# A two-block transformer step on one core: the last feature pair in token halves, with the final norm on all partitions

## The chip, the cores and the metric

The kernel runs on one core of one Trainium2 chip. The metric is the device time of one execution, in microseconds (us). Three runs of the kernel before took 2533.3, 2534.14 and 2535.93 us; the median is 2534.14 us.

## What is computed

Two blocks on 256 tokens of 2048 features. The first mixes tokens by forgetting attention and by an mLSTM, the second by a spatial gating unit and a gated linear recurrence (RG-LRU). Each is followed by a feed-forward net with a three-tap causal convolution, and each part adds its result to the residual stream x. The change touches only what comes last: the down projection of the second feed-forward net, its residual sum, and the final RMS norm.

```
def _rmsnorm(x, g):
    xf = x.astype(jnp.float32)
    y = xf * lax.rsqrt(jnp.mean(xf * xf, axis=-1, keepdims=True) + RMS_EPS)
    return (y * g.astype(jnp.float32)).astype(x.dtype)
...
    x = x + jnp.einsum('bsf,fd->bsd', jax.nn.gelu(gate) * val, ffn_w_down[l])
return _rmsnorm(x, final_g)
```

## The kernel before

x lies transposed on chip: features on the 128 partitions, tokens along the row. It is held as 8 feature pairs of [128, 2, 256] (two times 128 features, 256 tokens). All weights stream from memory once, in float32. `halves` (L193) loads 1 MB at a time on SP's queue and splits it: `hi` is the weight rounded to float32r by ScalarE (L207), `lo` the remainder by VectorE (L208). Operands are split the same way: a `Pair` holds [hi 256 | lo 256] columns for two tiles of the contraction. A block is four such tiles of weights; six blocks of hi and six of lo fit on chip (pool `wc`).

`proj_b` (L228) computes one output pair: for each tile k and each f of the two sets of 128 features, L239 multiplies hi weights with all 512 operand columns and L240 adds lo weights times the 256 hi columns. The result stands in PSUM as two halves of 256 columns whose sum is the product. Between blocks `tick` (L148) emits one step of each job that follows an earlier product, so that other engines work beside PE. Within an engine, instructions run in the order in which they are emitted (weights are emitted ahead of it).

`residual` (L667) runs eight products, one per output pair, and starts an `add_pair` job (L691) after each. In the last call, at the end of the second feed-forward net, the contraction has 24 tiles. `add_pair` copies one half out of PSUM (L698), adds both to x (L699, L700), squares the new x (L303) and adds the squares to `acc` on GpSimd (L309); for the last pair it also folds acc's two halves to 256 columns (L305 to L307). Then x is multiplied by the final gain (L712). `Norm.steps` (L311) sums acc over the partitions with a matmul by a column of ones, in token halves (L315), adds epsilon (L318), raises to the power -0.5 on GpSimd (L320), spreads the result along a diagonal (L325) and multiplies by ones, which puts the norm of each token on every partition (L326, copied at L328). `final` (L931) multiplies the eight pairs by it, five on VectorE (L939) and three on GpSimd (L937), and stores each with one transfer of 256 KB (L940), alternating between the queues of ScalarE and SP.

Of the kernel before, what the change touches and what calls it, by code (L numbers as in the profile page):

```python
# [9 lines left out]
AF = mybir.ActivationFunctionType  # L10
# [50 lines left out]
class Job:  # L61
    """Work that follows a matrix product, emitted in steps between later products."""

# [10 lines left out]
class Pair:  # L74
    """Two K tiles of an operand: [128, 2, hi 256 | lo 256], written by a job."""

# [4 lines left out]
class Builder:  # L81
# [17 lines left out]

# [1 line left out]
    def _name(self, s):  # L101
# [26 lines left out]
    @staticmethod  # L128
    def half(quads, j):
        """Feature pair j of x: [128, 2, 256]."""  # L130
        return quads[j // 2][:, 2 * (j % 2):2 * (j % 2) + 2, :]
# [4 lines left out]

# [1 line left out]
    def soon(self, gen):  # L138
# [9 lines left out]
    def tick(self):  # L148
        """Between blocks of a product: every urgent job that is due takes a step, and one other."""
        for j in list(self.urgent):  # L150
            if j.wait <= 0:
                j.step()
            else:
                j.wait -= 1
        took = False
        for j in list(self.later):
            if j.wait <= 0 and not took:
                j.step()
                took = True
            else:  # L160
                j.wait -= 1
        self.urgent = [j for j in self.urgent if not j.done]
        self.later = [j for j in self.later if not j.done]
# [9 lines left out]

# [1 line left out]
    def constants(self):  # L175
# [15 lines left out]

# [1 line left out]
    def halves(self, src):  # L193
        """src: [128, k tiles, columns] in DRAM. Yields per block of k tiles its (hi, lo) parts,
        float32r tiles whose sum is the float32 weight."""
        nc = self.nc
        nk, ncol = src.shape[1], src.shape[2]
        with self.tc.high_priority(offset=self.ahead):
            raw = self.raw.tile([P, nk, ncol], F32, tag="raw", name=self._name("raw"))
            nc.sync.dma_start(out=raw, in_=src)  # L200
            step = 1024 // ncol
            out = []
            for k0 in range(0, nk, step):
                kn = min(step, nk - k0)
                hi = self.wc.tile([P, kn, ncol], F32R, tag="wh", name=self._name("wh"))
                lo = self.wc.tile([P, kn, ncol], F32R, tag="wl", name=self._name("wl"))
                nc.scalar.copy(hi, raw[:, k0:k0 + kn, :])  # L207
                nc.vector.tensor_sub(lo, raw[:, k0:k0 + kn, :], hi.bitcast(F32))  # L208
                out.append([(hi[:, k, :], lo[:, k, :]) for k in range(kn)])
        return out  # L210

    def blocks(self, w, nk, first, before=None):
        """Loads the k tiles of w [128, nk, columns] piece by piece; yields blocks of parts."""
        k = 0
        size = 2048 // w.shape[2]
        sizes = list(first)
        while k < nk:
            n = min(sizes.pop(0) if sizes else size, nk - k)
            if before is not None:
                before(k, n)  # L220
            yield from self.halves(w[:, k:k + n, :])
            k += n
# [5 lines left out]
    def proj_b(self, w, pairs, first=(), before=None):  # L228
        """Transposed product with 256 weight columns, w [128, k tiles, 256]. PSUM [128, 2, 512];
        the product is the sum of its two 256-column halves."""  # L230
        nc = self.nc
# [14 lines left out]
    def proj_a(self, w, pairs):  # L246
        """Product with 512 weight columns, w [128, k tiles, 512], in token rows:
        PSUM [128 tokens, 2 halves, 512]."""
        nc = self.nc
# [24 lines left out]
    def split(self, dst, src, gains=None):  # L274
        """dst [128, 2, 512] float32r <- hi and lo parts of src [128, 2, 256] (times gains)."""
        nc = self.nc
# [10 lines left out]

# [1 line left out]
    class Norm:  # L289
        """1/rms per token of features that come in pairs [128, 2, 256]: r [128, 2] by token,  # L290
        bc [128, 256] on every partition."""

# [40 lines left out]
    def log1p_exp_neg_abs(self, x, t, e, w2, eng):  # L333
        """t = log(1 + exp(-|x|)) = 2 atanh(e / (2 + e)), e = exp(-|x|)."""
        nc = self.nc
# [12 lines left out]

# [1 line left out]
    def gates(self, pairs, norm):  # L350
        """Gate pre-activations, one row per head: 0-3 mLSTM forget, 4-11 forgetting attention,
        32-35 mLSTM input. Leaves what both recurrences need by token and by row."""
        nc = self.nc
# [64 lines left out]
    def qk_rows(self, ps, t, norm, g):  # L418
        """RMS norm over each head of 512 columns in token rows, then transposed to t."""
        nc = self.nc  # L420
# [24 lines left out]
    def rows_out(self, ps, out, c, norm, func, after=None):  # L445
        """512 columns in token rows: func(r * z)."""
        self.finish(norm.job)
        for m in range(2):
            s = slice(c * 512, (c + 1) * 512)
            self.nc.scalar.activation(out[m][:, s], ps[:, m, :], func, scale=norm.r[:, m:m + 1])  # L450
            if after is not None:
                self.nc.gpsimd.tensor_mul(out[m][:, s], out[m][:, s], after[:, s])
        yield 0
# [42 lines left out]
    def mlstm_head(self, h, q, k, v, gs, d, deps):  # L496
        """h_t = sum_s (q_t k_s) e^(a_s - c_t) v_s / max(|den|, e^-m_t), a = i - F, c = max(0, cummax a)."""
        nc = self.nc
# [45 lines left out]
    def first_operand(self, j, xs):  # L544
        """Pair j of x * gain from DRAM."""
        x = self.wk_tile([P, 2, S])
# [118 lines left out]

# [1 line left out]
    def residual(self, quads, w, groups, norm=None, gname=None, scales=None):  # L667
        """x += sum of operands @ w over groups (first k tile, pairs); w [8, 128, k tiles, 256].
        With norm, the new x's squares go to it and the pairs x * gain come back."""
        out = []  # L670
# [20 lines left out]
    def add_pair(self, quads, j, pss, scales, norm, gname, p):  # L691
# [16 lines left out]
        if norm is not None:  # L708
            norm.add(x, last=last)
            if p is None:  # L710
# [3 lines left out]

# [1 line left out]
    def ffn(self, quads, hx, norm, w_up, cw, cb, w_down, func, next_gain):  # L716
        nt = w_up.shape[0]
        npair = nt // 2
        for half in range(2):
# [10 lines left out]
            if half == 0:  # L730
                self.residual(quads, w_down, [(0, prods)])
        n = self.Norm(self, D)
        return self.residual(quads, w_down, [(2 * j0, prods)], n, next_gain), n

    def conv_pair(self, ps, y, norm, cw, cb, f0, nf, func=None):
        """Three-tap causal convolution over the tokens of two feature tiles."""
        nc = self.nc
# [20 lines left out]

# [1 line left out]
    def lru_scales(self):  # L760
        """-+ LRU_C * softplus(-lam) per channel."""
        nc = self.nc
# [33 lines left out]
    def lru_scan(self, xr, ra, ii, th, deps):  # L796
        """1 - a^2 = tanh(-log a) (1 + a^2); the state replaces xr."""
        nc = self.nc
# [131 lines left out]

    def final(self, quads, norm):  # L931
        nc, a = self.nc, self.a
        self.finish(norm.job)
        for j in range(8):
            x = self.half(quads, j)
            if j in (2, 5, 7):
                nc.gpsimd.tensor_mul(x, x, self.bc2(norm.bc))  # L937
            else:
                nc.vector.tensor_mul(x, x, self.bc2(norm.pb))  # L939
            (nc.sync if j % 2 else nc.scalar).dma_start(out=a["out"][:, 2 * j:2 * j + 2, :], in_=x)  # L940

    def build(self):
# [4 lines left out]
        hx, norm = self.mix2(x, hx, norm)  # L947
        _, norm = self.ffn(x, hx, norm, a["ffn_w_up_2"], "ffn_conv_w_2", "ffn_conv_b_2", a["ffn_w_down_2"],
                           AF.Gelu_apprx_tanh, None)
        self.finish_all()  # L950
        self.final(x, norm)

# [7 lines left out]
def _layout(i):  # L960
# [11 lines left out]
    def tiles(w, n):  # L972
        """[K, F] -> [F / n, 128, K / 128, n]"""
        w = np.asarray(w)
# [51 lines left out]
```

## Time and profile before

| what | us |
|---|---|
| median of three runs | 2534.14 |
| span of the profiled execution (first to last instruction) | 2531.7 |
| PE busy (share of the span) | 2485.9 (98%) |
| last pair's product, start to last matmul | 2497.58 to 2514.11 |
| rest of the program after it, to the span's end | 17.4 |

The profiled execution is one of its own; the page gives its span, which is 2.4 us under the median of the runs. Times in rows count from the span's start. PE is the matmul engine and PEld its weight loads, DVE is VectorE, ACT ScalarE, POOL GpSimd, SP SyncE; a q behind a name is that engine's queue of instructions, which issues transfers. A busy time of PE overlaps with the next matmul's, so steps are read from start to start. A float32 matmul leaves two records, a float32r matmul one. Idle time in square brackets is that of the engine before the instruction, with what ended it. The granted clock is a share of 2.4 GHz.

### The profile page before, as it was taken

The numbers are of one execution on the slowest core, as the hardware profiler recorded it, in microseconds if no ns is written. First come the engines' busy times: TensorE is split into PE (matmuls) and PEld (weight loads), VectorE is DVE, ScalarE is ACT, GpSimd is POOL, SyncE is SP. The second block draws the span as 40 slices with busy tenths as digits, with TensorE's granted clock in tenths as the row PEclk, the third lists the DMA queues.
The fourth block names the chain that finished last, engine by engine and source line by source line (L and its number), as shares of the span: only waits on it lengthen the run. The fifth ranks groups of instructions, "written<-read, shape, count | busy, mean of one in ns | idle before, by whom it ended". The sixth has DMA issues, their size and how long they took to land.

```text
span 2531.7 us, 34669 instructions
## 1 busy us (share of the span) xinstructions
PE 2485.9 (98%) x13926; PEld 2158.8 (85%) x13926; DVE 1630.0 (64%) x1938; ACT 1332.2 (53%) x1714; POOL 412.5 (16%) x326
## 2 busy tenths in 40 slices
PE   7999999999999999999999999999999999999997
PEld 6788888888888888888888878888888888888886
DVE  7555565577677764577665668777777645776643
ACT  5355474455555554455555564555555444555543
POOL 3412011111211110011111124241111100111111
PEclk9999999999999999999999999999999999999998
DMA  6454545565555555555555545555555555555552
GB/s 228 161 197 166 183 150 185 194 212 198 194 183 192 191 187 183 196 192 191 187 190 189 200 167 184 182 175 191 184 194 189 189 194 185 193 188 190 193 186 97
DMA packets 68442, 470.16 MB, mean 186 GB/s; under 512 B 7724, under 2 KB 7736, under 8 KB 14264
## 3 DMA queue, kind: packets, MB, share of 16 engines
q1 hardware_dynamic: 67392, 466.34, 53.6%
q8 instruction: 109, 1.79, 0.3%
q10 hardware_dynamic: 888, 1.60, 0.2%
q14 instruction: 53, 0.43, 0.0%
HBM read 465.80 MB, written 2.10 MB: 185 GB/s over the span
## 4 chain that ended last, share of the span: by engine, by line
PE 92%; DVE 3%; POOL 2%; issue 1%; ACT 1%; DMA 1%; SPq 0%; POOLq 0%; ACTq 0%; DVEq 0%
PE mm L239 54%; PE mm L240 27%; PE mm L261 3%; PE mm L259 3%; PE mm L260 3%; DVE wl L208 1%; ACT wh L207 0%; POOL act L705 0%; PE sm L792 0%; POOL act L345 0%; DVE wk L271 0%; POOL act L344 0%; DMA wk<-in_x 0%; DMA raw<-in_w_mqk 0%; POOL acc L309 0%
## 5 line engine op out<-in xcount | busy, mean ns | idle before, releaser
L239 PE MATMUL mm<-act,wh 128*128 128x512 f32 x6208 | 2168.5, 395 | 10.4 <-DVE act L284 5.4
L240 PE MATMUL mm<-act,wl 128*128 128x256 f32 x6208 | 1732.3, 279 | 2.2 <-DVE wl L208 2.2
L208 DVE TENSOR_TENSOR wl<-raw,wh 128x1024 fp32r<-128x1024 f32 (+1 forms) x882 | 1144.1, 1303 | 775.8 <-ACT wh L207 774.9
L207 ACT CAST wh<-raw 128x1024 fp32r<-128x1024 f32 (+1 forms) x882 | 916.3, 1042 | 941.8 <-PE mm L239 793.0
L239 PEld LDWEIGHTS mm<-act,wh 128*128 128x128 f32 x6208 | 1166.0, 188 | 277.0 <-ACT wh L207 8.2
L240 PEld LDWEIGHTS mm<-act,wl 128*128 128x128 f32 x6208 | 1172.1, 189 | 4.3 <-DVE wl L208 3.8
L740 POOL TENSOR_TENSOR wk<-wk,rbc 128x512 f32<-128x512 f32 x92 | 119.6, 1300 | 922.4 <-DVE wk L271 922.4
L261 PE MATMUL mm<-wl,act 128*128 128x512 f32 x384 | 151.0, 393 | 6.0 <-DVE wl L208 6.0
L746 DVE SCALAR_TENSOR_TENSOR wk<-wk,vecs,wk 128x255 f32<-128x255 f32 (+1 forms) x368 | 152.8, 473 | 4.2 <-ACT wk L744 4.1
L259 PE MATMUL mm<-wh,act 128*128 128x512 f32 x384 | 153.0, 398 | 2.4 <-ACT wh L207 2.4
L260 PE MATMUL mm<-wh,act 128*128 128x512 f32 x384 | 150.7, 392 | 0.0
L744 ACT ACTIVATE wk<-wk,vecs 128x256 f32<-128x256 f32 x184 | 100.8, 595 | 51.4 <-POOL wk L740 51.3
L700 POOL TENSOR_TENSOR act<-act,wk 128x512 f32<-128x512 f32 x35 | 45.6, 1302 | 437.4 <-DVE act L699 437.4
L271 DVE TENSOR_TENSOR wk<-wk,mm 128x512 f32<-128x512 f32 x156 | 106.1, 680 | 3.5 <-ACT wk L269 3.5
L261 PEld LDWEIGHTS mm<-wl,act 128*128 128x128 f32 x384 | 72.5, 189 | 23.3 <-DVE wl L208 8.1
L269 ACT COPY wk<-mm 128x512 f32<-128x512 f32 x156 | 90.0, 577 | 4.2 <-issue 2.3
L259 PEld LDWEIGHTS mm<-wh,act 128*128 128x128 f32 x384 | 72.5, 189 | 17.5 <-ACT wh L207 3.2
L260 PEld LDWEIGHTS mm<-wh,act 128*128 128x128 f32 x384 | 72.6, 189 | 14.6
L309 POOL TENSOR_TENSOR acc<-acc,wk 128x512 f32<-128x512 f32 x34 | 47.6, 1399 | 65.9 <-ACT wk L303 65.6
L650 POOL TENSOR_TENSOR act<-wk,rbc 128x512 f32<-128x512 f32 x16 | 22.7, 1421 | 211.1 <-DVE wk L271 211.1
L283 ACT ACTIVATE act<-act,vecs 128x256 fp32r<-128x256 f32 x48 | 21.8, 502 | 41.3 <-POOL act L700 20.5
L749 ACT ACTIVATE wk<-wk 128x512 f32<-128x512 f32 x46 | 29.1, 633 | 22.3 <-DVE wk L746 22.1
(210 smaller groups left out, 806.8 us busy)
## 6 DMA issues: line engine op xcount, KB each, us to landing
raw<-in_ffn_w_up SPq DMA_DIRECT2D x96, 1024.0 KB, 5.1
raw<-in_w_up SPq DMA_DIRECT2D x88, 1024.0 KB, 5.1
raw<-in_ffn_w_down SPq DMA_DIRECT2D x48, 1024.0 KB, 4.8
raw<-in_w_g SPq DMA_DIRECT2D x32, 1024.0 KB, 5.1
raw<-in_w_out SPq DMA_DIRECT2D x32, 1024.0 KB, 5.1
raw<-in_w_down SPq DMA_DIRECT2D x32, 1024.0 KB, 4.8
raw<-in_w_qkv SPq DMA_DIRECT2D x24, 1024.0 KB, 4.8
raw<-in_w_in SPq DMA_DIRECT2D x24, 1024.0 KB, 5.0
```

Of the source, the lines that this page charges most:

```text
L207: nc.scalar.copy(hi, raw[:, k0:k0 + kn, :])
L208: nc.vector.tensor_sub(lo, raw[:, k0:k0 + kn, :], hi.bitcast(F32))
L239: nc.tensor.matmul(ps[:, f, :], hi[:, f * P:(f + 1) * P], x, start=(k == 0), stop=False)
L240: nc.tensor.matmul(ps[:, f, 0:S], lo[:, f * P:(f + 1) * P], x[:, 0:S], start=False, stop=(k == nk - 1))
L259: nc.tensor.matmul(ps[:, m, :], xh, hi, start=(k == 0), stop=False)
L260: nc.tensor.matmul(ps[:, m, :], xl, hi, start=False, stop=False)
L261: nc.tensor.matmul(ps[:, m, :], xh, lo, start=False, stop=(k == nk - 1))
L269: nc.scalar.copy(tb, ps[:, :, S:2 * S])
L271: nc.vector.tensor_add(z, tb, ps[:, :, 0:S])
L740: nc.gpsimd.tensor_mul(z, z, self.bc2(norm.bc))
L744: nc.scalar.activation(y[:, i, :], z[:, i, :], AF.Identity, scale=tap(2), bias=self.vec(cb, f))
L746: nc.vector.scalar_tensor_tensor(y[:, i, q:], z[:, i, :S - q], tap(2 - q), y[:, i, q:], op0=ALU.mult, op1=ALU.add)
```

## The change

The last call of `residual` becomes `last_residual`. Seven pairs go as before, but `acc` keeps both of its halves. The last pair's product is computed twice, once for each 128 tokens (m = 0, 1), from the same split weights, which stay in their buffers: L753 with 2 x 128 operand columns (hi and lo of these tokens), L755 with 128. The first pass goes block by block as the weights come; the second runs over f, then k. Each token half is added to x by set of features (L761 to L763), and squared (L764).

The norm's sums now come from matmuls of all-ones [128, 128] weights with the squares: two parts of acc per token half (L803, both token halves after 16 of the 24 tiles of the second pass's first f) and two sets of the last pair's squares (L769). The sum of each token so stands on all partitions at once, [128 partitions, 128 tokens]. Epsilon is added there (L771) and GpSimd raises all of it to -0.5 (L773). VectorE multiplies all eight pairs of this token half (L782; the last pair with its gain, L779), and each is stored with a transfer of 128 KB (L783): the first half's on SP's queue, the second's on SP's and ScalarE's in turn. `final` and `Norm.steps` are no longer used here.

```
         if norm is not None:
-            norm.add(x, last=last)
+            norm.add(x, last=last and p is not None)
...
         n = self.Norm(self, D)
+        if next_gain is None:
+            return self.last_residual(quads, w_down, 2 * j0, prods, n)
         return self.residual(quads, w_down, [(2 * j0, prods)], n, next_gain), n
 
+    def last_residual(self, quads, w, k0, pairs, norm):
+        nc = self.nc
+        nk = 2 * len(pairs)
+        for j in range(7):
+            ps = self.proj_b(w[j][:, k0:k0 + nk, :], pairs)
+            job = self.soon(self.add_pair(quads, j, [ps], None, norm, None, None))
+        x = self.half(quads, 7)
+        parts = []
+
+        def product(ps, k, f, m):
+            t = self.operands(pairs, k).rearrange("p (c s) -> p c s", c=2)
+            hi, lo = parts[k]
+            ms = slice(m * P, (m + 1) * P)
+            nc.tensor.matmul(ps[:, f, 0:S].rearrange("p (c s) -> p c s", c=2), hi[:, f * P:(f + 1) * P],
+                             t[:, :, ms], start=(k == 0), stop=False)
+            nc.tensor.matmul(ps[:, f, 0:P], lo[:, f * P:(f + 1) * P], t[:, 0, ms],
+                             start=False, stop=(k == nk - 1))
+
+        def add(ps, f, m, sq):
+            xs = x[:, f, m * P:(m + 1) * P]
+            tb = self.wk_tile([P, P])
+            nc.scalar.copy(tb, ps[:, f, P:S])
+            nc.vector.tensor_add(xs, xs, ps[:, f, 0:P])
+            nc.vector.tensor_add(xs, xs, tb)
+            nc.scalar.activation(sq[:, f, :], xs, AF.Square)
+
+        def out(m, pn, sq):
+            ms = slice(m * P, (m + 1) * P)
+            for f in range(2):
+                nc.tensor.matmul(pn, self.ones[:, 0:P], sq[:, f, :], start=False, stop=(f == 1))
+            v = self.wk_tile([P, P])
+            nc.vector.tensor_scalar(v, pn, 1.0 / D, EPS, op0=ALU.mult, op1=ALU.add)
+            bc = self.wk_tile([P, P])
+            nc.gpsimd.tensor_tensor(bc, v, self.mhalf[:, 0:1].to_broadcast([P, P]), op=ALU.pow)
+            b2 = bc.unsqueeze(1).to_broadcast([P, 2, P])
+            for j in range(8):
+                y = self.half(quads, j)[:, :, ms]
+                if j == 7:
+                    for f in range(2):
+                        nc.vector.scalar_tensor_tensor(y[:, f, :], y[:, f, :], self.vec("final_g_2", 14 + f), bc,
+                                                       op0=ALU.mult, op1=ALU.mult)
+                else:
+                    nc.vector.tensor_mul(y, y, b2)
+                (nc.scalar if m and j % 2 == 0 else nc.sync).dma_start(out=self.a["out"][:, 2 * j:2 * j + 2, ms], in_=y)
+
+        pss = [self.mm_tile() for _ in range(2)]
+        pns = [self.sm_tile([P, P]) for _ in range(2)]
+        sqs = [self.wk_tile([P, 2, P]) for _ in range(2)]
+        for block in self.blocks(w[7][:, k0:k0 + nk, :], nk, ()):
+            parts += block
+            for k in range(len(parts) - len(block), len(parts)):
+                for f in range(2):
+                    product(pss[0], k, f, 0)
+            self.tick()
+        self.finish_all()
+        for f in range(2):
+            add(pss[0], f, 0, sqs[0])
+        for f in range(2):
+            for k in range(nk):
+                product(pss[1], k, f, 1)
+                if f == 0 and k == 15:
+                    for m in range(2):
+                        for h in range(2):
+                            nc.tensor.matmul(pns[m], self.ones[:, 0:P], norm.acc[:, h, m * P:(m + 1) * P],
+                                             start=(h == 0), stop=False)
+                    out(0, pns[0], sqs[0])
+            add(pss[1], f, 1, sqs[1])
+        out(1, pns[1], sqs[1])
...
-    def final(self, quads, norm):
...
-            if j in (2, 5, 7):
-                nc.gpsimd.tensor_mul(x, x, self.bc2(norm.bc))
-            else:
-                nc.vector.tensor_mul(x, x, self.bc2(norm.pb))
-            (nc.sync if j % 2 else nc.scalar).dma_start(out=a["out"][:, 2 * j:2 * j + 2, :], in_=x)
```

The order of instructions on DVE, from the end of the last pair's first pass on (act tiles are x, mm_21265 is the second pass's PSUM, sm_21266 and sm_21267 the two norm sums, wk_21455 and wk_21552 what the two pows write):

```order
L771 TENSOR_SCALAR wk_21453<-sm_21266 128x128
L782 TENSOR_TENSOR act_4213<-act_4213,wk_21455 128x2x128 x2
L782 TENSOR_TENSOR act_4415<-act_4415,wk_21455 128x2x128 x2
L782 TENSOR_TENSOR act_4617<-act_4617,wk_21455 128x2x128 x2
L782 TENSOR_TENSOR act_4819<-act_4819,wk_21455 128x2x128
L779 SCALAR_TENSOR_TENSOR act_4819<-act_4819,vecs,wk_21455 128x128 x2
L762 TENSOR_TENSOR act_4819<-act_4819,mm_21265 128x128
L763 TENSOR_TENSOR act_4819<-act_4819,wk_21490 128x128
L762 TENSOR_TENSOR act_4819<-act_4819,mm_21265 128x128
L763 TENSOR_TENSOR act_4819<-act_4819,wk_21543 128x128
L771 TENSOR_SCALAR wk_21550<-sm_21267 128x128
```

The nine multiplies of the first token half stand ahead of the four additions of the second. Before, DVE's order from the last pair's product on was:

```order
L699 TENSOR_TENSOR act_4819<-act_4819,mm_21264 128x512
L700 TENSOR_TENSOR act_4819<-act_4819,wk_21400 128x512
L306 TENSOR_TENSOR wk_21404<-wk_21404 128x256
L307 TENSOR_TENSOR acc_20480<-acc_20480,wk_21404 128x256
L318 TENSOR_SCALAR nv_21414<-sm_21411 128x2
L325 TENSOR_SCALAR dg_21419<-ident,nr_21416 128x128
L325 TENSOR_SCALAR dg_21422<-ident,nr_21416 128x128
L939 TENSOR_TENSOR act_4213<-act_4213,sm_21418 128x512 x2
L939 TENSOR_TENSOR act_4415<-act_4415,sm_21418 128x512
L939 TENSOR_TENSOR act_4617<-act_4617,sm_21418 128x512
L939 TENSOR_TENSOR act_4819<-act_4819,sm_21418 128x512
```

All of it came after the last matmul of the product, once for all 256 tokens. On POOL, the end of the order is now:

```order
L309 TENSOR_TENSOR acc_20480<-acc_20480,wk_21159 128x512
L700 TENSOR_TENSOR act_4819<-act_4819,wk_21296 128x512
L309 TENSOR_TENSOR acc_20480<-acc_20480,wk_21300 128x512
L773 TENSOR_TENSOR wk_21455<-wk_21453,mhalf 128x128
L773 TENSOR_TENSOR wk_21552<-wk_21550,mhalf 128x128
```

Behind the seventh pair's sums POOL has only the two pows, one after the other, each on [128, 128] where it was one on [128, 2].

## Rows read from the trace of the kernel before

**Rows 1.** The page: span, and PE's busy time, share and instructions.
```profile
span 2531.7 us, 34669 instructions
...
PE 2485.9 (98%) x13926; PEld 2158.8 (85%) x13926; DVE 1630.0 (64%) x1938; ACT 1332.2 (53%) x1714; POOL 412.5 (16%) x326
```

**Rows 2.** Busy time by stretch, all engines; last row PE alone: then granted clock, DMA.
```profile
2497.60:2514.30 16.70, 16.70 (x98) 14.42 (x96) 1.82 (x2) 3.07 (x5) 3.32 (x3) 1.00 0.00 1
2514.30:2522.00 7.70, 1.92 (x9) 1.45 (x8) 3.01 (x8) 2.49 (x5) 0.80 (x2) 0.80 0.00 0
...
2519.00:2522.00 3.00, 1.22 (x4) 0.50 0.00 0
```

**Rows 3.** PE's timeline (start, us, what) at the last product and after it.
```profile
2497.58 0.39 PE L239 MATMUL mm<-act,wh 128*128 128x512 f32 x1
2497.81 0.27 PE L240 MATMUL mm<-act,wl 128*128 128x256 f32 x1
2497.93 0.40 PE L239 MATMUL mm<-act,wh 128*128 128x512 f32 x1
...
2514.11 0.28 PE L240 MATMUL mm<-act,wl 128*128 128x256 f32 x1
2518.23 0.61 PE L315 MATMUL sm<-ones,acc 128*128 128x1 f32 x4 [3.84 <-DVE acc L307]
2520.20 1.22 PE L326 MATMUL sm<-dg,ones 128*128 128x128 f32 x4 [1.36 <-DVE dg L325]
```

**Rows 4.** The timeline of the other engines after the last product.
```profile
2514.42 0.58 ACT L698 COPY wk<-mm 128x512 f32<-128x512 f32 x1 [10.87 <-PE mm L240]
2515.04 0.69 DVE L699 TENSOR_TENSOR act<-act,mm 128x512 f32<-128x512 f32 x1 [14.47 <-ACT wk L698]
...
2519.11 0.71 POOL L320 TENSOR_TENSOR nr<-nv,mhalf 128x2 f32<-128x2 f32 x1 [14.32 <-DVE nv L318]
2519.85 0.48 DVE L325 TENSOR_SCALAR dg<-ident,nr 128x128 f32<-128x128 f32 x2 [0.82 <-POOL nr L320]
...
2521.46 0.37 ACT L328 COPY rbc<-sm 128x256 f32<-128x256 f32 x1 [3.40 <-PE sm L326]
2521.86 3.08 DVE L939 TENSOR_TENSOR act<-act,sm 128x512 f32<-128x512 f32 x5 [1.52 <-ACT rbc L328]
2521.91 3.72 POOL L937 TENSOR_TENSOR act<-act,rbc 128x512 f32<-128x512 f32 x3 [2.09 <-ACT rbc L328]
...
2524.43 3.10 SPq L940 DMA_DIRECT2D out_t<-act  x4
```

**Rows 5.** DVE's timeline: the last split of weights.
```profile
2498.75 1.23 DVE L208 TENSOR_TENSOR wl<-raw,wh 128x1024 fp32r<-128x1024 f32 x1 [1.55 <-ACT wh L207]
```

**Rows 6.** Timeline: weight loads of two records each, and sixteen records of 128 columns.
```profile
176.54 0.40 PEld L515 LDWEIGHTS sm<-ones,wk 128*128 128x128 f32 x2
...
177.95 0.30 PEld L519 LDWEIGHTS sm<-ones,wk 128*128 128x128 f32 x2
...
1546.98 1.95 PE L854 MATMUL sm<-act,act 128*128 128x128 f32 x16
```

**Rows 7.** Pow by line: duration in ns, minimum/median/maximum, first and last start.
```profile
L331 POOL TENSOR_TENSOR rq<-ss,mhalf x8: 1006/1007/1912, 205.7 to 275.4; 128x4 f32<-128x4 f32 x8
L331 POOL TENSOR_TENSOR hrn<-hss,mhalf x4: 688/696/742, 180.8 to 215.3; 128x2 f32<-128x2 f32 x4
L331 POOL TENSOR_TENSOR bnr<-bnv,mhalf x2: 548/1030/1512, 1523.5 to 1524.0; 128x1 f32<-128x1 f32 x2
L320 POOL TENSOR_TENSOR nr<-nv,mhalf x7: 707/708/1692, 28.6 to 2519.1; 128x2 f32<-128x2 f32 x7
```

**Rows 8.** Groups of instructions: busy us, mean ns of one; idle before.
```profile
L700 POOL TENSOR_TENSOR act<-act,wk 128x512 f32<-128x512 f32 x35 | 45.6, 1302 | 437.4 <-DVE act L699 437.4
...
L475 DVE SCALAR_TENSOR_TENSOR wk<-sm,gcols,act 128x128 f32<-128x128 f32 x8 | 2.8, 346 | 3.5 <-PE sm L470 3.5
```

**Rows 9.** Issues of transfers by line, after 2490 us: KB each, median us to landing; all eight.
```profile
out_t<-act SPq DMA_DIRECT2D x4, 256.0 KB, 3.6
...
DMA to landing us min/median/max: 2.7/3.6/4.6
```

More of the change, by code (lines that the diff above doesn't have):

```diff
@@ L929, in mix2 @@
         return self.residual(quads, a["w_out_2"], [(0, gm), (8, lr)], n2, "norm2_g_2", scales=[ngm, nlr]), n2
-    def final(self, quads, norm):
[L932 to L935, printed above, removed]
-            if j in (2, 5, 7):
-                nc.gpsimd.tensor_mul(x, x, self.bc2(norm.bc))
-            else:
-                nc.vector.tensor_mul(x, x, self.bc2(norm.pb))
-            (nc.sync if j % 2 else nc.scalar).dma_start(out=a["out"][:, 2 * j:2 * j + 2, :], in_=x)
     def build(self):
@@ L947, in build @@
         hx, norm = self.mix2(x, hx, norm)
[L948 to L951, printed above, removed]
+        self.ffn(x, hx, norm, a["ffn_w_up_2"], "ffn_conv_w_2", "ffn_conv_b_2", a["ffn_w_down_2"],
+                 AF.Gelu_apprx_tanh, None)
 @with_exitstack
```

## The prediction

> **What bounds the kernel now.** I read the page first. The span is 2531.7 us and PE is busy for 98% of it [rows 1], so anything that is won or lost must lie on PE's stream or outside it. Only the end of the program is edited, so the next view is the table by stretch: in the last feature pair's product (2497.6 to 2514.3) PE is busy without a gap at full clock while no DMA moves; after it there are 17.4 us in which PE does next to nothing [rows 2]. PE's timeline gives the product's start, 2497.58, its last matmul, 2514.11, and its step: one L239 (512 columns) and one L240 (256) take 0.347 us (2497.58 to 2497.93), 0.231 and 0.116, so 48 such steps are 16.6 us [rows 3]. The timeline of the other engines gives the tail as one chain: copy, two adds, squares, sums on PE, pow on POOL, two diagonals, PE again, copy, eight multiplies, eight stores, end [rows 4]. What must be seen there: its pow at L320 handles two elements per partition and takes 0.71 us, and the last multiply ends at 2525.63 (2521.91 + 3.72), 6.1 us before the span's end.
>
> **The change, part by part.**
>
> *Product in token halves.* Each of the 48 steps becomes two, with half the columns: L753 (256 columns) and L755 (128). L753 has L240's shape: 0.116 us. For L755 no float32r row with under 256 columns exists. Matmul records with one moving column still follow one another, as their weight loads do, 0.11 us apart (0.30 less 0.19, L519) and records with 128 columns likewise ((1.95 - 0.28) / 15 = 0.112, L854) [rows 6]. So 0.112 us is what loading 128 weight columns takes, and I take it for L755. Bounds: 0.058 if columns alone counted (128/512 of 0.231), and 0.215, the step behind a 256-column record of full float32 (0.40 less 0.19, L515) [rows 6], if a short float32r matmul ran at that type's rate (four times as slow per column). A pair of instructions is then 0.228 us, and 96 of them 21.9 us against 16.6. The Trainium skill ("TensorE: Matmul & The Clock Gate", Back-to-back issue gap) gives about 81 ns for a matmul of 128 columns with its own weights; by that, an estimate, the product would be some 3 us shorter than by my price; the rows, at 0.112, do not show it.
>
> Loading and splitting the weights: the last split of this pair's weights ends at 2499.98 (2498.75 + 1.23) [rows 5], 2.4 us into the product. The sixth block is first wanted after 5/6 of the first pass, at 2497.58 + 9.1 = 2506.7, so holding all six blocks costs nothing. If that cover were gone, each block would cost its cast and subtraction, 2.3 us.
>
> *Norm sums on all partitions.* L803 and L769 put twelve float32 records (six matmuls of two) in the second pass: 12 x 0.112 = 1.34 us on PE. They replace L315 and L326 in the tail (0.61 and 1.22 us) [rows 3] and with them the diagonals and the copy.
>
> *The pow.* This is the term that decides. Before, pow works on one value per token and partition; now L773 takes 128 elements per partition, on POOL, twice. Its rows: 1 element 548 ns, 2 elements 696 (707 at L320), 4 elements 1007 [rows 7]. That is (1007 - 548) / 3 = 153 ns for each further element and 0.395 us fixed. At 128 elements: 0.395 + 128 x 0.153 = 20.0 us each. Bounds: the slopes between neighbouring rows, 148 and 155.5 ns, give 19.3 and 20.3 us; from below, POOL's cheapest elementwise row (1302 ns for 512 elements, 2.5 ns each, L700) [rows 8] gives 0.395 + 0.33 = 0.72 us. I take 20.0: the three pow rows lie on one line, and the addition is another operation.
>
> *What waits behind it.* Both pows are on POOL, so the second cannot start before the first has ended. On DVE the nine multiplies of the first token half wait for the first pow, and the four adds of the second half (L762, L763) stand behind them in DVE's order. So squares, sums and the second pow all wait for the first pow, and PE's remaining 7.3 us cannot cover it. The first pow starts only 6.7 us before PE's end.
>
> *Stores.* Sixteen stores of 128 KB instead of eight of 256 KB. Eight of them go in the first half's turn and land during the second pow: nothing. The last: before, 6.1 us lay between the last multiply and the end; the last store's queue was still issuing the store before it, and landing takes 3.6 us in the median (2.7 to 4.6) [rows 9]. I take 5.3, with 4.2 (end of the last issue [rows 4] to the end of the span: 2531.7 - 2527.53) and 7.5 (6.1, and 1.4 more if rows of 512 B instead of 2048 made the shortest landing half as long again) as bounds.
>
> **The sum**, on the profiled execution's axis, in us:
> - 64 steps of 0.2275 from 2497.58: 2512.14 (48 of the first pass, 16 of the second);
> - twelve sum records, and 0.16 until the last result: 2513.64;
> - L771 0.39 (a 128-column read of PSUM is 346 ns, L475 [rows 8]) and 0.08 to POOL: 2514.1;
> - first pow 20.0: 2534.1;
> - DVE's nine multiplies: steps of 0.60 for 512 columns (3.08 less 0.68, over 4) and 0.20 for 128 (L325, 0.48 less 0.28) [rows 4] give 0.33 for 256; 7 x 0.33 + 2 x 0.20 + 0.1 = 2.8: 2536.9;
> - four adds of 0.35, a square 0.36: 2538.7;
> - two sum records, at half clock because PE has idled for 18 us (after some 5 us of near idleness the clock before was 0.50, that is 1.2 GHz [rows 2], and four such records took 1.22 us, L326 [rows 3]): 0.61 and 0.07 to start, 2539.3;
> - L771 0.39, 0.08, second pow 20.0: 2559.8;
> - multiplies 2.8: 2562.6; the end 5.3: **2567.9**.
>
> Against 2531.7 that is +36.2 us, 1.4%. The runs' median is 2534.14, 2.4 above the profiled span; so 2567.9 + 2.4 = **2570 us**. In general, with X for one pow: end = 2528.0 + 2X while the first pow is what DVE waits for; below X = 3.4 it is hidden beside the second pass, and the end is 2531.4 + X (PE's end 2520.9, copy 0.33, adds 0.7, square 0.36, sums 0.43, L771 0.39 and 0.08, then X, 2.8, 5.3). A measurement of this kernel can tell about 0.2%, 5 us, from no change; slower by that means X above 4.4 us, 31 ns an element.
>
> **Rivals.**
>
> *Pow costs per element what other POOL work costs* (no difference, 12%). X = 0.72 us: 2531.4 + 0.72 = 2532.1, in runs 2534.5: the tail's saving (PE's end to the span's end 11.6 us instead of 17.4) is eaten by the 5.2 and 1.3 us added on PE. For it: additions at 2.5 ns an element, and that a few elements may show only start-up. Against it: three pow rows rising by 148 to 155 ns an element, 60 times as much. It decides not slower as long as an element costs under 31 ns. The Trainium skill ("GPSIMD Engine Reference", Elementwise — side-by-side cycle accounting) states 2.6 cycles per element for two-input elementwise work, and would agree with this rival; the pow rows here contradict it for pow.
>
> *Pow is partly overlapped over long rows*, X between 4.4 and 17 us (9%): 2528.0 + 2X, in runs 2539 to 2564. For it: only short rows are seen. Against: no flattening from 1 to 4.
>
> *Short float32r matmuls run at the float32 rate* (slower still, 17%). L755 at 0.215: the first pow starts 64 x 0.103 = 6.6 us later, so 2577 in runs with X = 20. For: full float32 shows that rate; against: the 256-column float32r step shows none of it.
>
> *L755 costs its columns only and pow is cheap* (faster, 4%): 96 x 0.054 = 5.2 off the first rival gives 2529.3 in runs, the edge of a gain; the 0.112 us between weight loads speaks against it. That no route reaches further than this is why faster has so little.
>
> **How the numbers follow.** Forecast 58%, its own range 2566 to 2574 (X 0.7 down and 0.3 up, counted twice; the end 1.1 down and 2.2 up; small steps 1). With the three other cases: slower 58 + 17 + 9 = 84%, same 12%, faster 4%. The range 2552 to 2581 takes in forecast, the slow float32r and the upper part of the partly overlapped pow (X above 11), about 80%.
>
> **What would show it.** In the changed profile: L773 twice at about 20 us on POOL, back to back but for some 6 us of DVE, ACT and PE; DVE idle before the first L782 with POOL as releaser; L755 0.11 us apart from the next L753; PE's end near 2520.8 and the span's end 47 us later. The prediction is wrong if L773 takes under 5 us, if L762 of the second half runs before the first half's multiplies, or if L755 takes 0.06 or 0.21.

## The result and the profile after

The changed kernel takes **2580.35 us** in the median of four runs (2580.09 to 2580.74), the kernel before 2533.72 in runs beside it: a ratio of 1.0169, with a 95% interval of 1.0142 to 1.0196. It is slower, inside the predicted range of 2552 to 2581, and 10.4 us above the predicted 2570. Some runs, of the kernel before and of six of the seven experiments, are about 15 us longer, and the two profiles of such a run (e2 and e5) show PE's step at 353 ns instead of 347 in about the last third of the program, well ahead of the edited code. For that reason kernels are also compared below by the **last stretch**: from the start of the last split of weights (the last L208) to the end of the span, in one profiled execution each.

| | before | after |
|---|---|---|
| span of the profiled execution, us | 2531.7 | 2578.5 |
| start of the last L208, us | 2498.75 [rows 5] | 2501.15 |
| last stretch, us | 32.95 | 77.35 |

So 44.4 of the 46.8 us lie in the last stretch. The other 2.4 us were there before the last pair began. In the profiles of e1, e4 and e6 to e8, whose code up to there is the same, this start lies 1.0 to 3.8 us later than in the profile of before, and three runs of the kernel before alone lie 2.6 us apart, so I do not count it to the change; that is argued, not shown. The profiled execution of the changed kernel took 2580.57 us.

The page of the changed kernel: the span, and by engine the busy time, share and instructions.
```profile
span 2578.5 us, 34917 instructions
...
PE 2498.3 (97%) x14030; PEld 2178.5 (84%) x14030; DVE 1628.6 (63%) x1954; ACT 1332.6 (52%) x1717; POOL 447.1 (17%) x323
```
Against [rows 1], PE has 12.4 us more work and POOL 34.6 us more, with three instructions fewer. Neither alone makes 46.8, and work that runs beside other work adds nothing, so the waits have to be looked at.

The table by stretch of the changed kernel, columns as in [rows 2]: the product until PE stops, the stop, the last quarter of the product, the tail.
```profile
2499.99:2518.00 18.01, 18.01 (x158) 17.95 (x156) 3.27 (x7) 4.11 (x9) 3.80 (x3) 1.00 0.00 1
2518.00:2540.70 22.70, 0.09 (x2) 0.00 (x0) 3.16 (x10) 0.27 (x1) 19.50 (x1) 0.57 0.07 19
2540.70:2548.40 7.70, 7.65 (x50) 7.65 (x50) 0.29 (x1) 0.31 (x1) 0.00 (x0) 0.73 0.30 82
2548.40:2578.50 30.10, 0.76 (x4) 0.37 (x3) 3.83 (x12) 0.57 (x2) 20.72 (x1) 0.56 0.13 35
```
In two stretches POOL is what works (19.5 of 22.7 us, 20.7 of 30.1) and PE all but rests. What is new against [rows 2] is the third: PE finishes its product only *after* the first of them.

VectorE's and POOL's timeline of the changed kernel from the first token half's norm on (start, us, engine, line, what; idle before and who ended it).
```profile
2516.40 0.29 DVE L771 TENSOR_SCALAR wk<-sm 128x128 f32<-128x128 f32 x1 [3.11 <-PE sm L769]
2537.54 2.44 DVE L782 TENSOR_TENSOR act<-act,wk 128x256 f32<-128x256 f32 x7 [20.84 <-POOL wk L773]
2539.89 0.61 DVE L779 SCALAR_TENSOR_TENSOR act<-act,vecs,wk 128x128 f32<-128x128 f32 x2
2540.42 0.28 DVE L762 TENSOR_TENSOR act<-act,mm 128x128 f32<-128x128 f32 x1
2540.73 0.29 DVE L763 TENSOR_TENSOR act<-act,wk 128x128 f32<-128x128 f32 x1
2548.78 0.29 DVE L762 TENSOR_TENSOR act<-act,mm 128x128 f32<-128x128 f32 x1 [7.76 <-ACT wk L761]
...
2550.32 0.29 DVE L771 TENSOR_SCALAR wk<-sm 128x128 f32<-128x128 f32 x1 [0.92 <-PE sm L769]
2571.51 2.44 DVE L782 TENSOR_TENSOR act<-act,wk 128x256 f32<-128x256 f32 x7 [20.89 <-POOL wk L773]
2573.86 0.61 DVE L779 SCALAR_TENSOR_TENSOR act<-act,vecs,wk 128x128 f32<-128x128 f32 x2
```
```profile
2516.77 20.73 POOL L773 TENSOR_TENSOR wk<-wk,mhalf 128x128 f32<-128x128 f32 x1 [10.40 <-DVE wk L771]
2550.76 20.72 POOL L773 TENSOR_TENSOR wk<-wk,mhalf 128x128 f32<-128x128 f32 x1 [13.25 <-DVE wk L771]
```
Each pow takes 20.7 us, where the pow of before took 0.71 (L320, [rows 4]). VectorE idles 20.84 us while the first runs, then multiplies, and only then comes L762, the add of the second token half. Between the two pows POOL idles 13.25 us.

PE's timeline of the changed kernel: the first pairs, the sum records, and the place where PE stops.
```profile
2499.99 0.28 PE L753 MATMUL mm<-act,wh 128*128 128x256 f32 x1
2500.11 0.22 PE L755 MATMUL mm<-act,wl 128*128 128x128 f32 x1
2500.17 0.33 PE L753 MATMUL mm<-act,wh 128*128 128x256 f32 x1
2500.34 0.22 PE L755 MATMUL mm<-act,wl 128*128 128x128 f32 x1
2500.40 0.33 PE L753 MATMUL mm<-act,wh 128*128 128x256 f32 x1
...
2514.74 1.11 PE L803 MATMUL sm<-acc,ones 128*128 128x128 f32 x8
2515.68 0.61 PE L769 MATMUL sm<-wk,ones 128*128 128x128 f32 x4
...
2517.87 0.22 PE L755 MATMUL mm<-act,wl 128*128 128x128 f32 x1
2540.75 0.58 PE L753 MATMUL mm<-act,wh 128*128 128x256 f32 x1 [22.67 <-DVE act L762]
2541.14 0.31 PE L755 MATMUL mm<-act,wl 128*128 128x128 f32 x1
```
And its largest waits from 2499 us on (engine, what and line, waited for; us in total, times, longest).
```profile
DVE act L782 <- POOL wk L773: 41.7, 2, 20.9
...
PE mm L753 <- DVE act L762: 22.7, 1, 22.7
```
The second row is what the prediction did not see. The product of the second feature set for the second token half stands still for 22.67 us, and what releases it is L762: the VectorE add that *reads* the other feature set out of the same PSUM tile (`pss[1]`). That add stands behind the nine multiplies, and these behind the pow. When PE resumes, its clock is not full (0.73 over the stretch): the first nine pairs, 2540.75 to 2544.66, take 0.43 us each at a granted clock of 0.50 (1.2 GHz, the lower of the two levels), the others 0.23.

### The profile page after: what moved, and what is told of

It is laid out like the page before. It is cut to its first block, busy times and chain, and to the rows that moved or that the text cites. A ratio compares the mean times of both kernels' runs of the same rounds, so it can differ in the third digit from the quotient of the medians.

```text
span 2578.5 us, 34917 instructions
## 1 busy us (share of the span) xinstructions
PE 2498.3 (97%) x14030; PEld 2178.5 (84%) x14030; DVE 1628.6 (63%) x1954; ACT 1332.6 (52%) x1717; POOL 447.1 (17%) x323
## 4 chain that ended last, share of the span: by engine, by line
PE 91%; POOL 3%; DVE 2%; issue 1%; ACT 1%; POOLq 1%; DMA 1%; SPq 0%; ACTq 0%; DVEq 0%
PE mm L239 53%; PE mm L240 27%; PE mm L259 3%; PE mm L261 3%; PE mm L260 3%; DVE wl L208 1%; POOLq L1083 1%; POOL wk L773 1%; PE mm L753 1%; ACT wh L207 1%; PE sm L866 0%; POOL act L705 0%; DMA wk<-in_x 0%; POOL act L345 0%; POOL act L344 0%
## 5 line engine op out<-in xcount | busy, mean ns | idle before, releaser
L208 DVE TENSOR_TENSOR wl<-raw,wh 128x1024 fp32r<-128x1024 f32 (+1 forms) x882 | 1141.5, 1300 | 780.5 <-ACT wh L207 780.1
L650 POOL TENSOR_TENSOR act<-wk,rbc 128x512 f32<-128x512 f32 x16 | 22.7, 1421 | 211.1 <-DVE wk L271 211.1
L753 PE MATMUL mm<-act,wh 128*128 128x256 f32 x96 | 24.4, 354 | 22.7 <-DVE act L762 22.7
L773 POOL TENSOR_TENSOR wk<-wk,mhalf 128x128 f32<-128x128 f32 x2 | 41.4, 20724 | 23.7 <-DVE wk L771 23.7
```

## The experiments

Seven kernels were run. Each is the changed kernel with one thing altered, unless the text says otherwise.

**The second feature set in a PSUM tile of its own** (e1). If PE stops because of the shared tile, this alone must set it free; the norm's order is untouched.
```diff
+        extra = self.sm_tile([P, 2, S])
 ...
+            ps = ps if ps is pss[0] else (ps if f == 0 else extra)
```
(The second line stands in `product` and in `add`.)

> The changed kernel with a PSUM tile of its own for the second feature set of the second pass; nothing else moves. Theory: PE stops before that product because its first matmul waits for the VectorE addition that reads the other half of the same PSUM tile, and that addition stands behind the first token half's multiplies, which wait for the first pow. Then PE runs on at full clock, the product ends near 2523 us on the profile's axis, and the second pow starts some 7.4 us earlier: span 2578.5 - 7.4 = about 2571, runs about 2573. Rival (PE stands still for another reason, or the product is not on the path): span within 1 us of 2578.5.

Measured: 2573.91 us (2572.89 and 2574.93), 1.0129 of the kernel before (1.0063 to 1.0194); last stretch 70.4, 7.0 us shorter. POOL's timeline of this kernel:
```profile
2516.02 20.73 POOL L775 TENSOR_TENSOR wk<-wk,mhalf 128x128 f32<-128x128 f32 x1 [10.41 <-DVE wk L773]
2543.09 20.72 POOL L775 TENSOR_TENSOR wk<-wk,mhalf 128x128 f32<-128x128 f32 x1 [6.33 <-DVE wk L773]
```
and its table by stretch from 2517 us on:
```profile
2517.00:2523.50 6.50, 5.90 (x52) 5.75 (x50) 0.00 (x0) 0.27 (x1) 6.50 (x1) 1.00 0.01 3
2523.50:2540.00 16.50, 0.00 (x0) 0.00 (x0) 3.17 (x11) 0.00 (x0) 13.26 (x1) 0.53 0.10 27
```
Now PE does its 24 pairs beside the first pow at full clock, and POOL's idle time between the pows is 6.33 us instead of 13.25. So the shared tile is the cause of the stop, and the stop costs 7.0 us, not 22.7: the rest of it lay beside the pow anyway. The prediction described this kernel, not the changed one: its 2573.91 us lie in the forecast's own range of 2566 to 2574, the changed kernel's 2580.35 do not.

**The second half's adds ahead of the first half's multiplies** (e2). The norm step is split from `out`, and on VectorE the multiplies of the first half are pinned in program order behind the adds of the second.
```diff
-                    out(0, pns[0], sqs[0])
+                    bc0 = norm_of(0, pns[0], sqs[0])
 ...
-        out(1, pns[1], sqs[1])
+        bc1 = norm_of(1, pns[1], sqs[1])
+        out(0, bc0)
+        out(1, bc1)
```


> The changed kernel with all multiplies pinned behind the second token half's additions on VectorE; PSUM tiles as in the changed kernel. Theory (the multiplies of the first half block the second half on VectorE): PE waits only some 0.6 us, the second pow follows the first without a gap (2516.8 + 2 x 20.7 = 2558.3), then 3 us of multiplies and 4 us to the end: span about 2565, runs about 2567. Rival (GpSimd alone sets the end, wherever the multiplies stand): no change from 2578.5.

Measured: last stretch 64.1 us, 13.3 shorter; two runs, 2564.6 and 2581.16, the profiled one being the longer (last L208 at 2515.03). POOL's and VectorE's timeline of this kernel:
```profile
2530.65 41.42 POOL L773 TENSOR_TENSOR wk<-wk,mhalf 128x128 f32<-128x128 f32 x2 [10.41 <-DVE wk L771]
```
```profile
2540.35 0.29 DVE L771 TENSOR_SCALAR wk<-sm 128x128 f32<-128x128 f32 x1 [0.92 <-PE sm L769]
2551.42 2.63 DVE L787 TENSOR_TENSOR act<-act,wk 128x256 f32<-128x256 f32 x7 [10.78 <-POOL wk L773]
...
2572.11 2.44 DVE L787 TENSOR_TENSOR act<-act,wk 128x256 f32<-128x256 f32 x7 [17.53 <-POOL wk L773]
```
PE's wait for L762 is down to 0.68 us, with the shared tile still in place. The second pow's input is ready at 2540.64, in the middle of the first pow, and the two run back to back. So the order behind the first pow (the stopped PE and the queued adds together) is worth all of POOL's 13.25 us of idle time, and no more. What is left over the kernel before is 31.1 us, with POOL at work from the start of the first pow to the end of the second.

**Shorter pows** (e4). The pow takes 64 columns in the first half and 16 in the second, and the rest of the norm is copied from the mean square, so what is left out is the power of 64 and 112 columns.

> The changed kernel with pow on 64 of the 128 columns in the first token half and on 16 in the second; the other columns of the norm stay at the mean square, so the output is not the norm. Theory (a fixed price per element, 0.159 us from 4 to 128 elements): 10.6 us and 2.9 us, together 28 us less, span about 2550. Rival (price per instruction or per row of many elements): both near 20.7 us, no change.

Measured: 2559.69 us in the median of eight runs (2551.39 to 2568.73); span of the profiled execution 2551.8, last stretch 49.3, 28.1 shorter. POOL's timeline of this kernel:
```profile
2518.15 10.53 POOL L775 TENSOR_TENSOR wk<-wk,mhalf 128x64 f32<-128x64 f32 x1 [10.41 <-DVE wk L771]
2541.86 2.89 POOL L775 TENSOR_TENSOR wk<-wk,mhalf 128x16 f32<-128x16 f32 x1 [13.18 <-DVE wk L771]
```
From 16 to 64 elements the slope is (10.53 - 2.89) / 48 = 0.159 us, from 64 to 128 (20.72 - 10.53) / 64 = 0.159: the price per element does not fall over long rows. The pows lost 10.2 and 17.8 us, together 28.0, and the kernel 28.1. Both lie wholly on the path.

**The product in token halves alone** (e5). The kernel *before*, with only the last pair's product done in halves (both halves in each block's turn, tail unchanged).
```diff
+                    for m in range(2):
+                        ms = slice(m * P, (m + 1) * P)
+                        nc.tensor.matmul(ps[:, f, :].rearrange("p (c s) -> p c s", c=2)[:, :, ms],
+                                         hi[:, f * P:(f + 1) * P], t[:, :, ms], start=(k == 0 and m == 0), stop=False)
+                        nc.tensor.matmul(ps[:, f, ms], lo[:, f * P:(f + 1) * P], t[:, 0, ms],
+                                         start=False, stop=(k == nk - 1 and m == 1))
```


> The kernel before, with only the last pair's product in token halves (both halves one after the other from each loaded block; one PSUM tile, the norm, the multiplies and the stores as before). Theory (each weight load takes 0.116 us and bounds both matmuls): 96 x 0.2315 - 48 x 0.3467 = +5.6 us, runs about 2539.3. Rival (columns alone count): within 1 us of the kernel before.

Measured: last stretch 38.6 us, 5.6 longer than before; 2542.03 us in the median of ten runs (2541.0 to 2558.8), 1.0026 of before (0.9998 to 1.0055), which alone would not tell it from no change. PE's timeline of this kernel:
```profile
2518.48 0.34 PE L242 MATMUL mm<-act,wh 128*128 128x256 f32 x1
2518.65 0.23 PE L244 MATMUL mm<-act,wl 128*128 128x128 f32 x1
2518.71 0.33 PE L242 MATMUL mm<-act,wh 128*128 128x256 f32 x1
```
A pair takes 0.231 us (2518.48 to 2518.71 here, 0.2315 over longer stretches), 96 of them 22.2 us against 16.6 [rows 3].

**The same norm without pow** (e6). The kernel of e1 with a square root on ScalarE (first called early, on one element) and a reciprocal on VectorE in place of the pow.
```diff
-            nc.gpsimd.tensor_tensor(bc, v, self.mhalf[:, 0:1].to_broadcast([P, P]), op=ALU.pow)
+            nc.scalar.activation(v, v, AF.Sqrt)
+            nc.vector.reciprocal(bc, v)
```


> The changed kernel with a PSUM tile of its own for the second feature set (as in the first experiment) and, in place of pow on GpSimd, a square root on ScalarE (its table loaded early) and a reciprocal on VectorE. Measured from the start of the last split of weights (L208) to the end of the span: before 32.9 us, changed 77.4. Theory (pow and the stop of PE are all that made it slower; the rest of the change gives back in the tail what it adds on PE): with some 1.3 us for root and reciprocal the first half is hidden and the stretch is 22.4 us to PE's end and 10.5 behind it, about 33. Rival (the token halves or the stores cost more than the 5.6 us measured for the product): 38 or more.

Measured: 2537.08 us against 2535.89 before in the same series, 1.0011 (0.9983 to 1.0038): no difference that the runs can tell; last stretch 33.0. VectorE's timeline of this kernel:
```profile
2516.67 0.29 DVE L773 TENSOR_SCALAR wk<-sm 128x128 f32<-128x128 f32 x1 [3.10 <-PE sm L771]
2517.40 0.95 DVE L776 RECIPROCAL wk<-wk 128x128 f32<-128x128 f32 x1 [0.44 <-ACT wk L775]
2518.39 2.44 DVE L785 TENSOR_TENSOR act<-act,wk 128x256 f32<-128x256 f32 x7
...
2527.55 2.44 DVE L785 TENSOR_TENSOR act<-act,wk 128x256 f32<-128x256 f32 x7
```
From the mean square to the first multiply 1.7 us pass instead of 21.1. With e1 this closes the account of the last stretch: 77.4 less 7.0 (tile) less 37.4 (pow, and what queues behind it: e1 against e6) is 33.0, as in the kernel before. All else in the change nets to nothing: 5.6 us for the halves and 1.3 for the sum records against a tail that is shorter by 7.0 (from the product's end, about 2524.0, 10.4 us to the end; before 17.4).

**Feature halves, and all-partition sums** (e7, e8). Was there a version that wins? The product keeps full rows of 512 and 256 columns, runs all blocks for the first feature set and then, from the kept weights, for the second; the sums go to all partitions, root and reciprocal as in e6, six multiplies on VectorE and two on POOL, eight stores of 256 KB.

> The last pair by feature halves instead of token halves, from the same kept weights: all contraction tiles for the first 128 features, then for the second, each with full 512 and 256 columns, in PSUM tiles of their own; norm sums on all partitions; square root on ScalarE and reciprocal on VectorE; eight multiplies (two on GpSimd) and eight stores of 256 KB as before. Theory (what the change meant to save can be had without the short matmuls and the pow): no cost on PE but 0.9 us of sums, and the first half's residual hidden; last L208 to the end 29 to 30 us against 32.9 before, so 3 to 4 us less, runs 0.1 to 0.15% under the kernel before. Rival (the reciprocal of 256 columns or the stores take it back): 33 or more.

Measured: 2535.03 us, 0.9992 of before (0.9969 to 1.0014); last stretch 32.4. That missed: neither the 29 to 30 us expected nor the rival's 33. The groups of this kernel by shape, from 2518 us on (line, engine, what; busy us, mean ns of one; idle before):
```profile
L790 DVE TENSOR_TENSOR act<-act,wk 128x512 f32<-128x512 f32 x6 | 5.8, 1037 | 0.0
L790 POOL TENSOR_TENSOR act<-act,wk 128x512 f32<-128x512 f32 x2 | 3.4, 1733 | 15.9 <-DVE wk L787 15.9
```
The multiplies, 0.6 us apart in the kernel before, have a mean of 1.04 here; the second and third, beside POOL's two, took 1.75 and 1.74, the others 0.68 to 0.69. In the kernel before VectorE read the norm from PSUM (L939, [rows 4]); here both its inputs lie in SBUF, as POOL's do. The Trainium skill ("GPSIMD Engine Reference", Key points) says that POOL shares its SBUF interfaces with VectorE, with contention for VectorE instructions that have two SBUF inputs. e8 tests that: the reciprocal is written to PSUM, where VectorE's multiplies read it, and ScalarE copies it to SBUF for POOL.
```diff
+        pb = self.sm_tile([P, S])
+        nc.vector.reciprocal(pb, v)
         bc = self.wk_tile([P, S])
-        nc.vector.reciprocal(bc, v)
+        nc.scalar.copy(bc, pb)
```


> As the feature-half version, with the reciprocal written to PSUM, from where VectorE's multiplies read it, and a copy in SBUF for GpSimd's two. Theory (two of VectorE's multiplies took 1.75 us instead of 0.68 because both their inputs lay in SBUF while GpSimd multiplied): all six take 0.68, steps of 0.60, GpSimd's two 1.27 each; last L208 to the end 32.4 - 2.1 = about 30.3 us. Rival (GpSimd and VectorE slow each other whatever memory the operand lies in): 32 or more, with multiplies of 1.75 us again.

Measured: 2533.91 us, 0.9988 of before (0.9963 to 1.0013); last stretch 31.9. VectorE's and POOL's timeline of this kernel:
```profile
2519.84 1.76 DVE L787 RECIPROCAL sm<-wk 128x256 f32<-128x256 f32 x1 [0.48 <-ACT wk L785]
2522.04 3.68 DVE L795 TENSOR_TENSOR act<-act,sm 128x512 f32<-128x512 f32 x6 [0.44 <-ACT wk L789]
```
```profile
2522.09 2.50 POOL L793 TENSOR_TENSOR act<-act,wk 128x512 f32<-128x512 f32 x2 [16.28 <-ACT wk L789]
```
The multiplies run at full pace again on both engines (3.68 us for six, 2.50 for two), so the contention is confirmed and the page agrees. But the kernel gained only 0.4 us from it and missed the 30.3 expected: the last multiply ends 1.9 us earlier (2525.72 against 2527.60), and 6.0 us follow it instead of 4.6. The rate of the transfers shows what follows, in GB/s by 40 slices from 2490 to 2533 us, first the kernel before, then this one:
```profile
GB/s 8 0 0 0 0 0 0 0 0 0 0 0 0 0 0 15 0 0 0 0 0 0 0 0 0 0 0 0 0 0 0 110 385 373 383 374 326 8 0 0
GB/s 0 8 0 0 0 0 0 0 0 0 0 0 0 0 0 0 15 0 0 0 0 0 0 0 0 0 0 0 0 0 0 50 381 372 389 372 383 6 8 0
```
Eight stores of 256 KB are 2.1 MB, and at some 380 GB/s they take 5.5 us, an estimate from these slices, however soon the last multiply ends; all 16 DMA engines are busy meanwhile (share 1.02 to 1.06 from 2525 to 2529 in e8). What counts then is when the first store is issued, and that is 2523.39 in e8 against 2523.61 in e7. This is read from the traces; no run tests it. One microsecond of the last stretch is gained on the kernel before, too little to be told from none in the runs: no version that beats both was found.

## Why the prediction came out as it did

**Right: the term that decides.** Pow takes the time its three short rows gave, on POOL, twice in series, on the path: e4 shows a price per element that holds from 16 to 128, and a kernel that pays all of it. The rival of a cheap pow is out by a factor of 29 (20.73 against 0.72), and the partly overlapped one by e4's equal slopes. The size was a little off: 0.159 us per element instead of 0.153, 0.73 us for each pow.

**Right: the pair.** 0.2315 us against 0.2275. My sign for it was ill chosen, though: I wrote that L755 at 0.06 would refute it, and on PE's rows the next L753 does start 0.06 behind L755, while L755 starts 0.17 behind L753. Only the pair can be read. If columns alone counted, it would be 0.116 + 0.058 = 0.174; at the float32 rate 0.331. PE's weight loads in the changed kernel keep the same pace, one load each 0.11 to 0.12 us whatever the matmul's columns, so that a pair takes as long as two loads; that the loads set the pace is argued from this:
```profile
2499.99 0.19 PEld L755 LDWEIGHTS mm<-act,wl 128*128 128x128 f32 x1
2500.11 0.19 PEld L753 LDWEIGHTS mm<-act,wh 128*128 128x128 f32 x1
2500.22 0.19 PEld L755 LDWEIGHTS mm<-act,wl 128*128 128x128 f32 x1
```
The Trainium skill's 81 ns for such a matmul ("TensorE: Matmul & The Clock Gate", Back-to-back issue gap) is not reached here, and the 3 us that it would have given back did not come.

**Wrong: "PE's remaining 7.3 us" beside the first pow.** That step took PE's second feature set as free to run. It followed what squares, sums and the second pow wait for behind the multiplies, but not what PE waits for: the add that stands in the same queue reads the PSUM tile that PE writes next. From the first multiplies' end to the second pow I had 2.9 us; 10.26 passed (2540.50 to 2550.76), since 7.5 us of product lie in there, 1.8 of them (nine pairs of 0.43) because PE's clock was low after the stop. With a tile of its own (e1) the same stretch is 3.3. The sign that the prediction gave, PE's end near 2520.8 and the span's end 47 us later, came out as 2548.2 and 30.

**Luck: the range.** The forecast's own range was 2566 to 2574, and 2580.35 lies outside it. It falls inside 2552 to 2581 by 0.65 us, because the upper end was set for short float32r matmuls at the float32 rate, which did not happen; the 7.4 us that were missed took the room kept for them.

**The sum, closed.** Measured less predicted, in us: start of the last pair +2.4 (not counted to the change); its way to the first pow +0.3; the two pows +1.45; the two rounds of multiplies +0.4; between them and the second pow +7.4; the end -1.3 (4.0 from the last multiply instead of 5.3; 3.9 to 4.0 in e1, e2 and e6). Together 10.6, which is 2578.5 less 2567.9. The stores bear on why the end was shorter; issues by line of the changed kernel from 2490 us on:
```profile
out_t<-act SPq DMA_DIRECT2D x12, 128.0 KB, 2.0
out_t<-act ACTq DMA_DIRECT2D x4, 128.0 KB, 2.5
```
A store of half the size lands in 2.0 to 2.5 us in the median, against 3.6 [rows 9], and only 1.05 MB are left to store behind the second pow, where before it was all 2.1. The rate is lower: 283 to 288 GB/s from 2573 to 2576 us, against 373 to 385 in the full slices of the kernel before. The bound of 7.5 had counted a slower landing of the shorter rows, but not that half of the bytes were gone by then. One sum of the first rival does not come out either: its terms add up to 11.1 us from PE's end, not 11.6; its 2532.1 does not use the 11.6.

**Right: weights kept on chip, and the stores of the first half.** PE ran the first pass and half of the second without a gap (18.01 of 18.01 us busy, 156 of the 158 matmul records being its 72 pairs and the twelve sums), and the stores of the first half cost nothing. They landed earlier than predicted, though: by the rate of the transfers (GB/s, 40 slices from 2490 to 2579 us) they were under way from about 2539 to 2544, beside the rest of the product, and nothing moved while the second pow ran.
```profile
GB/s 15 4 0 0 0 0 0 7 0 0 0 0 0 0 0 0 0 0 0 0 0 3 242 227 7 0 0 0 0 0 0 0 0 0 0 0 0 207 264 4
```

## What to carry to other kernels

A function that costs nothing on two elements may decide the end of a kernel on 128: price it per element from rows of several sizes, and multiply. When an instruction waits long, go through all that is queued behind it on its engine and ask of each not only who needs its result, but also who waits to overwrite what it reads; a PSUM tile shared by two products made TensorE wait for VectorE here. Cutting a matmul's columns in half doubles the weight loads, and here a pair of short matmuls took as long as its two loads. And before speeding up the last multiplies, look whether the stores behind them already run at full rate.

## What the runs showed of the hardware

- Pow on POOL is a straight line: 2.89, 10.53 and 20.73 us for 16, 64 and 128 elements per partition, that is 0.35 + 0.159 per element. Square root on ScalarE and reciprocal on VectorE for the same 128 took 0.31 and 0.95 us; the reciprocal of 256 took 1.75.
- Float32r matmuls of 256 and 128 columns, each with its own weights, took 0.231 us a pair, as long as two weight loads of 0.115; nothing of the float32 rate (0.215, [rows 6]) showed.
- After 22.7 us of idleness PE's pairs took 0.43 us instead of 0.23 for the first 3.9 us, at a granted clock of 0.50 (1.2 GHz, the lower of the two levels), and that added 1.8 us to a product of 5.6.
- A VectorE multiply with both inputs in SBUF took 1.75 us instead of 0.68 beside a POOL multiply, and POOL's own 1.70 to 1.76 instead of 1.27; with one input in PSUM neither was slowed (e7, e8).
- Stores of 256 KB ran at 372 to 389 GB/s (e8), stores of 128 KB in rows of 512 bytes at 283 to 288 (changed kernel).
